# Later sums for two weights, and earlier copies out of one bank, in a hybrid attention and convolution layer

## The chip, the cores and the metric

The kernel runs on one core of a Trainium2 chip. Its engines are TensorE (PE, with PEld its weight loads), VectorE (DVE), ScalarE (ACT), GpSimd (POOL) and SyncE (SP); each runs its own instructions in a fixed order and waits on semaphores for the others. 16 DMA engines move data for all queues. The metric is the time of one execution in microseconds (us), the median of several runs.

## The reference

One layer on x of 512 tokens by 2048 channels, float32, cut to what matters:

```python
h = rmsnorm(x, g_pre)
q, k, v, z_att, u, g_glu, z_conv = split(h @ w_in)   # each 512 x 1024
# 8 heads x 128: stick-breaking attention, strictly causal
z = q k^T / sqrt(128)
a = exp(log_sigmoid(z) + sum over s<j<t of -softplus(z))
y_att = (a @ v) * silu(z_att)
# convolution module, 1024 channels
c = causal_depthwise_conv31(u * sigmoid(g_glu)) + conv_b
y_conv = (silu(layernorm(c)) @ w_pw2 + b_pw2) * silu(z_conv)
y = concat(y_att, y_conv) @ w_out                    # 2048 x 2048
out = x + rmsnorm(y, g_post)
```

## The kernel before

**Products.** Each float32 operand is split into an upper and a lower part (`split`, lines 101 to 111): ScalarE rounds a tile to its upper part (line 104), DVE subtracts (line 105). A product is three matmuls: upper by upper, upper by lower, lower by upper. Weights come in tiles of 1 MB: `r_` is the raw tile loaded by SyncE, `h_` its upper and `l_` its lower part, two buffers of each. A raw buffer is free for the load after next when DVE has made `l_`.

**Steps.** The work behind the start is a list of 96 steps, numbered from 0. A step has one weight tile and two units of matmuls; while a step runs, the next one's load and split are put into the program ahead of it. Steps 0 to 9 are u, q, k, g and u; 10 to 23 are v (12 matmuls in a unit); 24 to 49 are the rest of q, k, u, g and the gates za (24 matmuls in a unit), with the 8 heads of attention between their units; 50 to 63 are zc; 64 to 67 the pointwise product; 68 to 95 the output product. TensorE's order is written out by hand. The order on the other engines comes from a scheduler that places each instruction by its priority and by when it expects its inputs.

**Seven products for eight.** v, zc and the output product are cut in 2 x 2 blocks and done in 7 products in place of 8. Four of the seven need sums of weight blocks. GpSimd has them made in DRAM by DMA alone (`plan_sums`, lines 514 to 534): a transfer that copies one block (line 528) and one that accumulates another onto it (line 524). They are 1 MB each: 16 for v (`vs`), 16 for zc (`zs`) and 32 for w_out (`ws`). The last two lists are taken in turn from one queue, `sumq`.

**When a sum goes.** `sum_next` (line 536) issues the next transfer of a list and makes it wait for the latest matmul so far. For zc and w_out the constants of line 50 and these lines say how many are issued, at most one behind each unit:

```python
        if SUMS_FROM <= n < n_zc - 1 or n >= n_in:
            due += SUMS_A_STEP
```

Here n is the step, n_zc is 50 and n_in is 64. The queue of GpSimd is in order, so an instruction behind such a transfer waits until TensorE has come that far. Besides sums GpSimd runs the selects of attention (line 698, two groups of four for each head, `t1` and `t3`) that TensorE's transposes `aT` (line 742) need, additions of convolution channels (`ln_sum`, line 426) and small memsets.

**The end of v.** Steps 18 to 23 are the products 3, 7 and 4, in that order, two steps each; r_v30, r_v31, r_v70, r_v71, r_v40 and r_v41 are their weights. Products 7 and 4 use the same two PSUM banks, `va0` and `va1`. So when product 7 is done, `v_done` (line 608) has ScalarE copy each bank to SBUF (`v_a0`, `v_a1`, line 621), and TensorE may not begin product 4 in a bank before its copy is done. Step 24 is the first of q, with `r_q10`; step 25 has `r_q11`.

Of the kernel before, what the change touches and what calls it, by code (L numbers as in the profile page):

```python
# [46 lines left out]
    ("hl", 1), ("hl", 2), ("hl", 3),  # L47
]

SUMS_FROM, SUMS_A_STEP = 20, 1.5  # L50


@with_exitstack
def hybrid_layer(
# [15 lines left out]
    nc = tc.nc  # L70
# [18 lines left out]
    def t2(name, dt=F32):  # L89
        return t2p.tile([P, S], dt, tag="t2", name=name)  # L90
# [413 lines left out]
    def v_keep(chunk, m, src):  # L504
        a, b = t2(f"v_hi{chunk}_{m}", F32R), t2(f"v_lo{chunk}_{m}", F32R)
        v_hi[chunk, m], v_lo[chunk, m] = a, b
        split(a, b, src)
# [53 lines left out]
    v_form, v_ps, v_part = {}, {}, {}  # L561
# [46 lines left out]
    def v_done(q, i):  # L608
        ps = v_ps[q, i]
        tt = nc.vector.tensor_tensor  # L610
        if q in (1, 5, 6):
            v_part[q, i] = t2(f"v_part{q}_{i}")
            nc.scalar.copy(v_part[q, i], ps)
            return
        if q == 4:
            v_keep(0, 2 + i, ps)
            return
        c = v_part[{2: 1, 3: 6, 7: 5}[q], i]
        if q == 7:
            ps = t2(f"v_a{i}")  # L620
            nc.scalar.copy(ps, v_ps[q, i])
        if q == 2:
            tt(out=c, in0=ps, in1=c, op=ALU.add)
        elif q == 3:
            tt(out=c, in0=ps, in1=c, op=ALU.subtract)
        else:
            tt(out=c, in0=c, in1=ps, op=ALU.subtract)
        v_keep(0 if q == 2 else 1, i if q in (2, 3) else 2 + i, c)
# [18 lines left out]
    def v_unit(q, kg, i):  # L647
        def go(w):
            hi, lo = w
            if q == 2 and kg == 0:  # L650
                v_ps[q, i] = trp.tile([P, S], F32, tag="tr", name=f"vc{i}")
            elif kg == 0:
                v_ps[q, i] = {
                    1: lambda: mm(f"va{i}"), 5: lambda: mm(f"vb{i}"), 6: lambda: v_ps[1, i],
                    3: lambda: v_ps[5, i], 7: lambda: v_ps[1, i], 4: lambda: v_ps[1, i],
                }[q]()
            ps = v_ps[q, i]
            for k in range(4):
                ah, al = v_stationary(q, kg * 4 + k, i)
                st, en = q in (1, 2, 5) and kg + k == 0, kg == 1 and k == 3  # L660
                nc.tensor.matmul(ps, ah, hi[:, k, :], start=st, stop=False, skip_group_check=True)
                nc.tensor.matmul(ps, ah, lo[:, k, :], start=False, stop=False, skip_group_check=True)
                latest[0] = nc.tensor.matmul(
                    ps, al, hi[:, k, :], start=False, stop=en, skip_group_check=True
                ).ins
            if kg == 1:
                with tc.high_priority(offset=LATER):
                    v_done(q, i)
        return go
# [811 lines left out]
```

## Time and profile before

| | |
|---|---|
| median of 3 runs | 865.88 us (864.94 to 866.87) |
| the profiled execution | 864.89 us, of which its span is 863.2 |
| TensorE busy | 849.9 us (98%) |
| DVE, ScalarE, GpSimd busy | 658.0, 417.1, 142.8 us |
| mean granted TensorE clock | 0.996 |
| DMA queue of SyncE (q1) | 120.74 MB, 40.1% of 16 engines' span |
| DMA queue of GpSimd, the sums (q0) | 69.21 MB, 33.5% |

In a row of the order of time stand the start and the duration in us, engine, line, operation, output <- inputs, how many were merged, and in brackets how long the engine sat idle before it and what released it. Buffer numbers are left out of names there: `h_v` is any upper part of v's weights. A waits row reads: engine, tile and line that waited, what for, us in total, times, longest.

### The profile page before, as it was taken

What the parts mean: (1) busy time and instruction counts of PE and PEld (TensorE: products, weight loads), DVE (VectorE), ACT (ScalarE), POOL (GpSimd) and SP (SyncE); (2) the same over time, 40 slices, a digit from 0 to 9 for tenths busy, and PEclk for the clock granted to TensorE, in tenths of its full rate; (3) what the DMA queues carried; (4) which work ended last, traced back from release to release, by engine and by line L of the source; (5) the groups of instructions that cost most, each with busy time, mean ns of one, the idle gap of its engine ahead of it and who ended that gap; (6) DMA issues with size and microseconds to landing.
All of it is one profiled execution on the core that took longest, in us unless ns stands there. A gap on an engine that the chain in (4) does not pass through costs nothing.

```text
span 863.2 us, 9933 instructions
## 1 busy us (share of the span) xinstructions
PE 849.9 (98%) x3872; PEld 703.4 (81%) x3872; DVE 658.0 (76%) x791; ACT 417.1 (48%) x475; POOL 142.8 (17%) x170
## 2 busy tenths in 40 slices
PE   9999999999989999999999999999999999999996
PEld 6888888888868888888888888888888888888885
DVE  5799989689969669779898974368974776458774
ACT  5784222146444344333533545459853356455543
POOL 0111010200013131322313154230000100000031
PEclk9999999999999999999999999999999999999999
DMA  8798985856797889757698868937755995556783
GB/s 322 236 289 218 306 185 204 194 187 219 259 340 227 243 189 201 245 150 240 190 221 152 267 204 173 278 125 288 282 204 201 208 257 217 196 196 251 286 287 101
DMA packets 92278, 195.04 MB, mean 226 GB/s; under 512 B 3702, under 2 KB 46210, under 8 KB 86856
## 3 DMA queue, kind: packets, MB, share of 16 engines
q1 hardware_dynamic: 66688, 120.74, 40.1%
q0 software_dynamic: 22304, 69.21, 33.5%
q10 hardware_dynamic: 3240, 4.46, 1.6%
q8 instruction: 30, 0.49, 0.2%
q14 instruction: 16, 0.13, 0.0%
HBM read 186.01 MB, written 75.50 MB: 303 GB/s over the span
## 4 chain that ended last, share of the span: by engine, by line
PE 85%; DVE 8%; ACT 3%; DMA 2%; issue 1%; POOL 0%; DVEq 0%; ACTq 0%; POOLq 0%
PE q L353 3%; PE q L351 3%; PE q L352 3%; PE a L1091 3%; PE a L1092 3%; PE a L1090 3%; PE za L351 3%; PE za L353 3%; PE za L352 3%; PE u L351 3%; PE k L351 3%; PE k L353 3%; PE u L352 3%; PE k L352 3%; PE u L353 3%; DVE acc L410 2%
## 5 line engine op out<-in xcount | busy, mean ns | idle before, releaser
L410 DVE SCALAR_TENSOR_TENSOR acc<-hg,vec,acc 128x512 f32<-128x512 f32 x240 | 180.1, 750 | 6.6
L105 DVE TENSOR_TENSOR l_w<-r_w,h_w 128x2048 fp32r<-128x2048 f32 x28 | 64.2, 2292 | 42.2 <-ACT h_w L104 42.2
L104 ACT ACTIVATE h_w<-r_w 128x2048 fp32r<-128x2048 f32 x28 | 53.6, 1915 | 42.5 <-DMA r_w<-ws 12.7
L353 PE MATMUL q<-h_hi,l_q 128*128 128x512 f32 x128 | 50.8, 396 | 1.6 <-DVE l_q L105 1.6
L351 PE MATMUL q<-h_hi,h_q 128*128 128x512 f32 x128 | 50.6, 396 | 1.0 <-ACT h_q L104 1.0
L351 PE MATMUL u<-h_hi,h_u 128*128 128x512 f32 x128 | 50.3, 393 | 0.5 <-DVE k_lo L105 0.5
L352 PE MATMUL q<-h_lo,h_q 128*128 128x512 f32 x128 | 50.3, 393 | 0.0
L351 PE MATMUL k<-h_hi,h_k 128*128 128x512 f32 x128 | 50.1, 392 | 0.0
L351 PE MATMUL za<-h_hi,h_za 128*128 128x512 f32 x128 | 50.1, 391 | 0.0
L353 PE MATMUL k<-h_hi,l_k 128*128 128x512 f32 x128 | 49.9, 390 | 0.0
L353 PE MATMUL za<-h_hi,l_za 128*128 128x512 f32 x128 | 49.9, 390 | 0.0
L353 PE MATMUL u<-h_hi,l_u 128*128 128x512 f32 x128 | 49.9, 390 | 0.0
L352 PE MATMUL za<-h_lo,h_za 128*128 128x512 f32 x128 | 49.8, 389 | 0.0
L352 PE MATMUL k<-h_lo,h_k 128*128 128x512 f32 x128 | 49.8, 389 | 0.0
L352 PE MATMUL u<-h_lo,h_u 128*128 128x512 f32 x128 | 49.8, 389 | 0.0
L1092 PE MATMUL a<-h_w,f_lo 128*128 128x512 f32 x128 | 49.8, 389 | 0.0
L1091 PE MATMUL a<-l_w,f_hi 128*128 128x512 f32 x128 | 49.8, 389 | 0.0
L1090 PE MATMUL a<-h_w,f_hi 128*128 128x512 f32 x128 | 49.8, 389 | 0.0
L698 POOL TENSOR_SCALAR_AFFINE_SELECT t<-t 128x128 f32<-128x128 f32 x64 | 36.0, 596 | 74.2 <-DVE t L721 46.0
L105 DVE TENSOR_TENSOR l_z<-r_z,h_z 128x2048 fp32r<-128x2048 f32 x14 | 32.1, 2292 | 17.0 <-ACT h_z L104 16.9
L104 ACT ACTIVATE h_v<-r_v 128x2048 fp32r<-128x2048 f32 x14 | 26.8, 1915 | 37.2 <-PE u L352 17.5
L105 DVE TENSOR_TENSOR l_v<-r_v,h_v 128x2048 fp32r<-128x2048 f32 x14 | 33.0, 2361 | 13.0 <-ACT h_v L104 13.0
(381 smaller groups left out, 2246.5 us busy)
## 6 DMA issues: line engine op xcount, KB each, us to landing
ws<-in_w_out_dram POOLq DMA_DIRECT2D x24, 1024.0 KB, 9.6
r_w<-ws SPq DMA_DIRECT2D x16, 1024.0 KB
vs<-in_w_in_dram POOLq DMA_DIRECT2D x12, 1024.0 KB, 10.4
zs<-in_w_in_dram POOLq DMA_DIRECT2D x12, 1024.0 KB, 10.2
r_w<-in_w_out_dram SPq DMA_DIRECT2D x12, 1024.0 KB
r_u<-in_w_in_dram SPq DMA_DIRECT2D x8, 1024.0 KB
r_q<-in_w_in_dram SPq DMA_DIRECT2D x8, 1024.0 KB
r_k<-in_w_in_dram SPq DMA_DIRECT2D x8, 1024.0 KB
```

Source lines behind the costliest of these rows:

```text
L104: nc.scalar.activation(hi, src, AF.Copy)
L105: made = nc.vector.tensor_tensor(out=lo, in0=src, in1=f32(hi), op=ALU.subtract)
L351: nc.tensor.matmul(ps, wh, ah, start=first, stop=False)
L352: nc.tensor.matmul(ps, wh, al, start=False, stop=False)
L353: latest[0] = nc.tensor.matmul(ps, wl, ah, start=False, stop=last).ins
L410: bgq.append(lambda j=j: nc.vector.scalar_tensor_tensor(out=acc, in0=hg[:, j : j + S], scalar=vec[:, ct, j : j + 1], in1=acc, op0=ALU.mult ...
L698: nc.gpsimd.affine_select(out=blk, in_=blk, compare_op=ALU.is_gt, fill=0.0, base=0, pattern=[[-1, P]], channel_multiplier=1,)
L1090: nc.tensor.matmul(ps, fh[:, kk, ts], hi[:, k, :], start=st, stop=False, skip_group_check=True)
L1091: nc.tensor.matmul(ps, fh[:, kk, ts], lo[:, k, :], start=False, stop=False, skip_group_check=True)
L1092: nc.tensor.matmul(ps, fl[:, kk, ts], hi[:, k, :], start=False, stop=en, skip_group_check=True)
```

## The change

Two constants: the sums of zc and w_out begin with step 22 in place of 20, and 1.625 are due in a step in place of 1.5, which is 13 in 8 steps in place of 12. And the two copies v_a are given a high priority.

```diff
-SUMS_FROM, SUMS_A_STEP = 20, 1.5
+SUMS_FROM, SUMS_A_STEP = 22, 1.625
...
         if q == 7:
             ps = t2(f"v_a{i}")
-            nc.scalar.copy(ps, v_ps[q, i])
+
+            with tc.high_priority(offset=3000):
+                nc.scalar.copy(ps, v_ps[q, i])
```

The sums issued in a step, from line 1429 and at most one behind each unit:

| step | 20 | 21 | 22 | 23 | 24 | 25 | 26 | 27 | 28 | 29 | 30 | 31 |
|---|---|---|---|---|---|---|---|---|---|---|---|---|
| before | 1 | 2 | 1 | 2 | 1 | 2 | 1 | 2 | 1 | 2 | 1 | 2 |
| now | 0 | 0 | 1 | 2 | 1 | 2 | 2 | 1 | 2 | 2 | 1 | 2 |

By the end of step 48 both have issued 43; the last 5 follow from step 64 on.

GpSimd from the end of v's sums to the second head. `zs500` is the sum for product 5 of zc, first half of columns, first tile; `ws510` that of w_out, second half. Before:

```order
L524 DMA vs401_1274<-in_w_in_dram 512x1x512
L528 DMA zs500_1919<-in_w_in_dram 512x1x512
L528 DMA ws500_1960<-in_w_out_dram 512x1x512
L528 DMA zs501_1982<-in_w_in_dram 512x1x512
L528 DMA ws501_2003<-in_w_out_dram 512x1x512
L426 TENSOR_TENSOR ln_sum_1374<-ln_sum_1374,acc2_1433 128x512
L401 MEMSET hg4_2531 128x30
L524 DMA zs500_1919<-in_w_in_dram 512x1x512
L528 DMA ws510_2059<-in_w_out_dram 512x1x512
L524 DMA zs501_1982<-in_w_in_dram 512x1x512
L698 AFFINE_SELECT t1_0_2118<-t1_0_2118 128x128 x4
L528 DMA ws511_2206<-in_w_out_dram 512x1x512
```

Now, in the same place:

```order
L524 DMA vs401_1274<-in_w_in_dram 512x1x512
L426 TENSOR_TENSOR ln_sum_1374<-ln_sum_1374,acc2_1433 128x512
L401 MEMSET hg4_2529 128x30
L528 DMA zs500_1997<-in_w_in_dram 512x1x512
L528 DMA ws500_2035<-in_w_out_dram 512x1x512
L528 DMA zs501_2054<-in_w_in_dram 512x1x512
L528 DMA ws501_2099<-in_w_out_dram 512x1x512
L700 AFFINE_SELECT t1_0_2114<-t1_0_2114 128x128 x4
L524 DMA zs500_1997<-in_w_in_dram 512x1x512
L700 AFFINE_SELECT t3_0_2115<-t3_0_2115 128x128 x4
L528 DMA ws510_2235<-in_w_out_dram 512x1x512
```

The addition and the memset have moved ahead of the first sum, and three sums that stood ahead of head 0's first selects now stand behind them.

ScalarE at the end of v, from the first copy out of product 7's banks to the splits of q's first two weights. Before:

```order
L621 COPY v_a0_1953<-va0_1477 128x512
L104 ACTIVATE v_hi1_2_1956<-v_part5_0_1693 128x512
L104 ACTIVATE h_v41_1986<-r_v41_1985 128x2048
L621 COPY v_a1_1975<-va1_1491 128x512
L104 ACTIVATE v_hi1_3_1978<-v_part5_1_1708 128x512
L104 ACTIVATE h_q10_2020<-r_q10_2019 128x2048
L104 ACTIVATE v_hi0_2_2037<-va0_1477 128x512
L104 ACTIVATE h_q11_2074<-r_q11_2073 128x2048
```

Now:

```order
L623 COPY v_a0_1951<-va0_1477 128x512
L104 ACTIVATE v_hi1_2_1954<-v_part5_0_1693 128x512
L104 ACTIVATE h_v41_1980<-r_v41_1979 128x2048
L623 COPY v_a1_1971<-va1_1491 128x512
L104 ACTIVATE v_hi1_3_1974<-v_part5_1_1708 128x512
L104 ACTIVATE h_q10_2014<-r_q10_2013 128x2048
L104 ACTIVATE v_hi0_2_2031<-va0_1477 128x512
L104 ACTIVATE h_q11_2069<-r_q11_2068 128x2048
```

Nothing moved here: only line and buffer numbers differ. TensorE's and SyncE's rows are the same throughout as well. On DVE the lower part of a weight trades places with the scans of a head (line 729, now 731) in heads 1, 4 and 5, and in 4 and 5 one small operation goes ahead of the head's subtraction (line 733, now 735).

## The prediction

> **What bounds the kernel now.** I read the page first, then the list of waits for TensorE, then the stretch of the program where most of that waiting lies: TensorE, ScalarE, GpSimd and the SyncE queue in order of time, and last the traffic of the DMA queues microsecond by microsecond.
>
> ```profile
> span 863.2 us, 9933 instructions
> PE 849.9 (98%) x3872; PEld 703.4 (81%) x3872; DVE 658.0 (76%) x791; ACT 417.1 (48%) x475; POOL 142.8 (17%) x170
> PE idle L1284 <- POOL mean_w L140: 1.8, 1, 1.8
> PE va L661 <- ACT v_a L621: 1.7, 1, 1.7
> PE q L353 <- DVE l_q L105: 1.6, 1, 1.6
> PE last L1160 <- ACT diag L1159: 1.5, 1, 1.5
> PE q L351 <- ACT h_q L104: 1.0, 1, 1.0
> PE u L351 <- DVE k_lo L105: 0.5, 1, 0.5
> ```
>
> TensorE is busy for 98% of the span, so only its own waits can shorten the kernel, and there are six. The first and the fourth are the program's start and its last block. Three of the other four (v_a, h_q, l_q) lie within 12 us of each other, where the last two steps of v pass into the first step of q:
>
> ```profile
> 236.34 0.39 PE L661 MATMUL va<-h_v,h_hi 128*128 128x512 f32 x1
> 238.83 0.39 PE L663 MATMUL va<-h_v,h_lo 128*128 128x512 f32 x1
> 240.88 0.50 PE L661 MATMUL va<-h_v,h_hi 128*128 128x512 f32 x1 [1.66 <-ACT v_a L621]
> 250.36 0.50 PE L351 MATMUL q<-h_hi,h_q 128*128 128x512 f32 x1 [1.03 <-ACT h_q L104]
> 252.69 0.79 PE L353 MATMUL q<-h_hi,l_q 128*128 128x512 f32 x1 [1.59 <-DVE l_q L105]
> 253.28 0.63 PE L351 MATMUL q<-h_hi,h_q 128*128 128x512 f32 x1
> 253.71 0.63 PE L352 MATMUL q<-h_lo,h_q 128*128 128x512 f32 x1
> 256.40 0.39 PE L353 MATMUL q<-h_hi,l_q 128*128 128x512 f32 x1
> ```
>
> From start to start a product takes (238.83 - 236.34) / 11 = 0.226 us here. Between 238.83 and 256.40 stand 48 products (three units of v of 12, and 12 of q), which is 10.87 us at that pace and took 17.57. So this place loses **6.7 us**: 240.88 - 238.83 - 0.23 = 1.8 us at v_a, and 4.9 us at h_q, l_q and in the products behind them, which come 0.43 us apart (253.28 to 253.71) before the pace returns. Why were they late?
>
> ```profile
> 230.28 0.32 SPq L639 DMA_DIRECT2D r_v<-vs  x1
> 235.42 0.38 SPq L336 DMA_DIRECT2D r_q<-in_w_in_dram  x1
> 236.03 0.63 ACT L104 ACTIVATE v_hi<-v_part 128x512 fp32r<-128x512 f32 x1 [1.62 <-DVE v_part L627]
> 238.44 1.91 ACT L104 ACTIVATE h_v<-r_v 128x2048 fp32r<-128x2048 f32 x1 [1.78 <-DMA r_v<-vs]
> 240.26 0.57 ACT L621 COPY v_a<-va 128x512 f32<-128x512 f32 x1
> 248.40 1.91 ACT L104 ACTIVATE h_q<-r_q 128x2048 fp32r<-128x2048 f32 x1 [3.45 <-DMA r_q<-in_w_in_dram]
> ```
>
> Both roots are loads. The last weights of v were issued at 230.28 and split from 238.44 on; the copy v_a that TensorE needs stood behind that split on ScalarE. The first weights of q were issued at 235.42 and split from 248.40, 13 us later. What lay between are the sums that GpSimd issues:
>
> ```profile
> 228.65 0.76 POOL L528 DMA_DIRECT2D zs<-in_w_in_dram  x1 [61.38 <-PE va L663]
> 234.09 0.73 POOL L528 DMA_DIRECT2D ws<-in_w_out_dram  x1 [4.68 <-PE va L663]
> 236.80 0.70 POOL L528 DMA_DIRECT2D zs<-in_w_in_dram  x1 [1.98 <-PE va L663]
> 239.52 0.70 POOL L528 DMA_DIRECT2D ws<-in_w_out_dram  x1 [2.02 <-PE va L663]
> 240.15 1.37 POOL L426 TENSOR_TENSOR ln_sum<-ln_sum,acc 128x512 f32<-128x512 f32 x1
> ```
>
> The DMA view of single microseconds shows who moved data (packets, MB, share of the 16 engines). The rows are those of the microsecond from 231 (one), 234 (one), 237 (two), 240 (its larger one), 243 (two); q0 carries the sums, q1 SyncE's loads.
>
> ```profile
> q0 software_dynamic: 94, 0.39, 95.3%
> ...
> q1 hardware_dynamic: 47, 0.39, 104.0%
> ...
> q0 software_dynamic: 96, 0.39, 97.4%
> q1 hardware_dynamic: 5, 0.02, 5.9%
> ...
> q1 hardware_dynamic: 357, 0.37, 102.6%
> ...
> q0 software_dynamic: 97, 0.38, 92.6%
> q1 hardware_dynamic: 42, 0.04, 10.7%
> ```
>
> They take turns, nearly whole: the load of v issued at 230.28 gets nothing in 231, all of 234, and its last packets wait in 237 behind the second sum; the load of q gets 240 and then a tenth of 243. A load alone is 1.05 MB / 0.37 to 0.39 MB per us = 2.7 to 2.8 us.
>
> **The change, part by part.** *Copies.* The two v_a copies are to be moved ahead on ScalarE. ScalarE's rows at this place are the same in both programs: the second copy still stands behind the split of the last weights of v. This part adds, removes and moves nothing; cost and gain 0. If the wait at v_a goes, it goes because the load is early.
>
> *Sums, start.* By the two constants, steps 20 to 23 issued 1, 2, 1 and 2 sums and now issue 0, 0, 1 and 2. A unit of v is 2.7 us, so the first sum moves from 228.65 to the end of the first unit of step 22, 239.06, the second to about 244.5, the third to 247.2, the fourth into the first step of q. The 228.65, 234.09 and 236.80 transfers are then gone from the time in which both late loads run.
>
> - Load of v, issued 230.28 as before (its buffer comes free by DVE, which is untouched): alone it lands near 234 to 235. Its split may then start when ScalarE is done with v_hi, at 236.03 + 0.63 = 236.66, not 238.44. Everything behind shifts by 1.78 us: TensorE resumes at 240.88 - 1.78 = 239.10, where its own pace asks for 239.06. Bounds: 0 to 1.8 us remain; I take 0.05, since no sum stands in front of the load any more.
> - Load of q, issued 235.42: alone about 3 us and a start of one or two, so 239 to 241; at worst 248.4 as before. The nearest row is that of 240, the load alone, since the first sum is now issued after it. ScalarE reaches h_q at about 242.1 (it must first split a part of v that waits for DVE), then 1.9 and 2.3 us for h_q and l_q: 246.4. TensorE comes to q at 239.06 + 3 x 2.72 = 247.2 and needs l_q 0.45 us later. Covered by 1 us; if the load landed later than 243 that cover is gone.
> - The products at 0.43 us come only behind the waits, so they go with them. The Trainium skill, "TensorE: Matmul & The Clock Gate" (What's actually happening), says that the array halves its clock after an idle window of about 3.4 us and regains it after as long a busy one. The 0.43 us rows agree, and so does the single wait at 240.88 without them; by that rule a remaining wait of 1 or 2 us would cost itself and no slow stretch.
>
> *Sums, rate.* 13 in 8 steps for 12: by step 48 both programs have issued 43. In between each comes up to two and a half steps later, and nobody reads one before the steps of zc. A copy moves 0.39 MB in a microsecond, 2.7 us; an accumulation half of that:
>
> ```profile
> q0 software_dynamic: 96, 0.20, 109.2%
> 252.66 6.19 SPq L336 DMA_DIRECT2D r_k<-in_w_in_dram  x2
> 266.71 1.92 ACT L104 ACTIVATE h_k<-r_k 128x2048 fp32r<-128x2048 f32 x1 [1.38 <-PE q L352]
> ```
>
> (the row is of the microsecond from 252, an accumulation: 5.2 us for a sum). Per step of about 12 us that is 2.8 us of load and 1.5 sums of 2.7 to 5.2 us, now 1.6: under 11.3 us. The load of k issued at 252.66 was wanted at 266.71, when TensorE freed the buffer, 14 us later, and had landed by then although the four sums shown above were issued in the 24 us ahead of it. Loads in these steps have twice the room of v's. Cost 0, hidden by that room.
>
> *GpSimd's queue.* The addition ln_sum moves from behind the fourth sum to ahead of the first, so from 240.15 to about 237, when DVE has finished its input. There it no longer runs beside l_v, which took 3.29 us; beside the small v_lo it meets nothing that TensorE waits for. The selects of each head now stand behind other sums. A sum holds the queue until TensorE has passed its unit, so I compared that unit with the time each select is ready: for all 16 groups the unit ends first, by under 1 us at the closest. Head 0's second group, the first to get an accumulation ahead of it, is ready near 270.4, and that sum is let go near 265.6.
>
> ```profile
> 277.02 3.18 POOL L698 TENSOR_SCALAR_AFFINE_SELECT t<-t 128x128 f32<-128x128 f32 x4 [3.37 <-ACT t L734]
> 283.06 1.14 PE L742 MATMUL aT<-ident,t 128*128 128x128 f32 x9
> 240.39 3.29 DVE L105 TENSOR_TENSOR l_v<-r_v,h_v 128x2048 fp32r<-128x2048 f32 x1 [2.99 <-ACT h_v L104]
> ```
>
> *DVE.* In heads 1, 4 and 5 a weight's lower part changes places with scans. That costs a head at most the rest of a split and one operation of 512 columns, an estimate of 1.5 us from the 1.91 and 0.63 of such on ScalarE. Head 0 had 283.06 - 280.20 = 2.9 us to spare ahead of its transposes, and I take the others to be like it. In head 0 TensorE no longer waits while DVE catches up, so DVE is there about 1 us later relative to TensorE (two l of 2.3 us and 13 taps have to follow each other); that still fits. What is late next is k_lo (0.5 us), which stays.
>
> **Sum.** 6.7 - 0.05 - 0.05 for rounding = 6.6 us. The profiled execution took 864.89 us, its span 863.2 and 1.7 around it; 864.9 - 6.6 = 858.3. It lay 1.0 us under the median of the three runs, 865.88, so the median should be **859.3 us**, 0.76% faster. A measurement of this kernel can tell about 0.2%, 1.7 us.
>
> **Rivals.**
> 1. *v_a still waits.* The copy has not moved, so any lateness of v's last load or its split keeps the 1.8 us: 859.3 + 1.8 = 861.1. For it: the 1.78 us is TensorE's to lose at the least delay. Against it: the rows of 231 and 237, where the sums alone hold the load up. The Trainium skill, "DMA: Bandwidth & Descriptors" (Queues, rings and completion order), says that each engine goes round-robin between its queues packet by packet. By an even share the load of v would have landed near 237 beside the sums, in time for ScalarE, the 1.8 us would have another cause, and the sum would be 861.1; the rows of 231 and 234 speak against an even share.
> 2. *DVE is the next bound.* TensorE arrives 6.6 us earlier, DVE only in part: if head 0's chain slips by 5 us instead of 1, its transposes wait 2 us: 861.3. Against it: DVE waited 2.99 us at 240.39, idleness that it gets back.
> 3. *The wait moves to q.* If the first sum at 239.06 still cuts off the tail of q's load, 4.9 us stay and only 1.8 go: 864.1, at the edge of no change; with 1 us more elsewhere, none. Against it: 3.6 us between the two issues, where the load needs 2.8.
> 4. *Slower.* The denser accumulations (five in steps 28 to 31) make loads late within attention. A late load there costs what q's did, 4.9 us; two make 859.3 + 9.8 = 869.1. It decides when a load lands some 20 us after its issue (14 us to the split, 6 more to its use), so three accumulations of 5.2 us and its own 2.8 in a row do not reach it; their units lie 5.4 us or more apart.
>
> **Chances.** Forecast 0.63; rival 1 0.12; rival 2 0.10; rival 3 0.09; rival 4 0.06. Faster by over 0.2%: the forecast, rivals 1 and 2 and a third of rival 3, 0.88. Same: the rest of rival 3, 0.06. Slower 0.06. The range goes from 857.9 (k_lo's 0.5 also gone, and a low run) to 862.5, past rivals 1 and 2 and short of 3 and 4.
>
> **What would show it.** In the changed kernel's waits v_a, h_q and l_q are gone or under 0.3 us each; q0 is silent until about 240; v's last split starts near 236.7, and q's first near 242; no products 0.43 us apart; ScalarE's order as before. The step most likely to be wrong is q's load landing by 243, or a transpose of a head that now waits for a select on GpSimd: either would stand as a new row among TensorE's waits.

## The result, and the profile after

The changed kernel takes **857.71 us** (median of 4 runs, 857.53 to 858.60), the kernel before in the same series 866.18 us (4 runs, 864.94 to 866.87). The ratio is **0.9906**, with a 95% interval of 0.9889 to 0.9923: 8.5 us faster (6.7 to 9.6), where 6.6 were forecast. The time lies 1.6 us under the 859.3 us that were forecast, and 0.2 us under the lower end of the forecast's range, 857.9. (The kernel before came out at 866.18 us here, 0.3 us above the 865.88 from which the forecast started.) The profiled execution of the changed kernel took 858.60 us.

First the head of the page, then TensorE's waits:

```profile
span 856.9 us, 9933 instructions
PE 847.4 (99%) x3872; PEld 702.0 (82%) x3872; DVE 654.3 (76%) x791; ACT 416.8 (49%) x475; POOL 146.4 (17%) x170
PE idle L1286 <- POOL mean_w L140: 1.8, 1, 1.8
PE last L1162 <- ACT diag L1161: 1.5, 1, 1.5
PE gn L493 <- ACT h_hi L252: 0.7, 1, 0.7
PE u L351 <- DVE k_lo L105: 0.5, 1, 0.5
```

The rows of v_a, h_q and l_q are gone. The row of gn is new; it lies in the program's start, 21 us in (e1 below has 0.4 us there, the others none), and it shifts everything in this execution by some 0.7 us. So the rows that follow stand about 0.75 us later than rows of before would. In order of time, SyncE's queue, ScalarE and GpSimd at the end of v and the start of q:

```profile
231.03 0.32 SPq L641 DMA_DIRECT2D r_v<-vs  x1
236.16 5.83 SPq L336 DMA_DIRECT2D r_q<-in_w_in_dram  x2
236.77 0.63 ACT L104 ACTIVATE v_hi<-v_part 128x512 fp32r<-128x512 f32 x1 [1.62 <-DVE v_part L629]
237.33 1.92 ACT L104 ACTIVATE h_v<-r_v 128x2048 fp32r<-128x2048 f32 x1
239.16 0.56 ACT L623 COPY v_a<-va 128x512 f32<-128x512 f32 x1
242.87 1.92 ACT L104 ACTIVATE h_q<-r_q 128x2048 fp32r<-128x2048 f32 x1
249.79 1.92 ACT L104 ACTIVATE h_q<-r_q 128x2048 fp32r<-128x2048 f32 x1 [3.60 <-DMA r_q<-in_w_in_dram]
237.54 1.74 POOL L426 TENSOR_TENSOR ln_sum<-ln_sum,acc 128x512 f32<-128x512 f32 x1 [69.51 <-DVE acc L410]
240.27 0.76 POOL L528 DMA_DIRECT2D zs<-in_w_in_dram  x1 [0.93 <-PE va L665]
```

The split of v's last weights follows v_hi at once, and the first split of q's weights has no brackets: neither waits for its load now. The copy v_a still stands behind the split, as before, and is early enough. The queues, in the microseconds from 234, 239, 240, 241 and 243:

```profile
q1 hardware_dynamic: 53, 0.42, 98.6%
...
q1 hardware_dynamic: 369, 0.38, 107.6%
...
q1 hardware_dynamic: 194, 0.18, 52.1%
...
q0 software_dynamic: 13, 0.05, 46.4%
...
q0 software_dynamic: 100, 0.41, 102.4%
```

Both loads have the engines to themselves, and the first packets of a sum come in 241, when q's load is through. TensorE passes the place at its pace of 0.23 us, without the products 0.43 us apart:

```profile
247.83 0.39 PE L665 MATMUL va<-h_v,h_lo 128*128 128x512 f32 x1
248.06 0.39 PE L351 MATMUL q<-h_hi,h_q 128*128 128x512 f32 x1
248.51 0.39 PE L353 MATMUL q<-h_hi,l_q 128*128 128x512 f32 x1
```

### The profile page after: what moved, and what is told of

It is laid out like the page before. It is cut to its first block, busy times and chain, and to the rows that moved or that the text cites. A ratio compares the mean times of both kernels' runs of the same rounds, so it can differ in the third digit from the quotient of the medians.

```text
span 856.9 us, 9933 instructions
## 1 busy us (share of the span) xinstructions
PE 847.4 (99%) x3872; PEld 702.0 (82%) x3872; DVE 654.3 (76%) x791; ACT 416.8 (49%) x475; POOL 146.4 (17%) x170
## 4 chain that ended last, share of the span: by engine, by line
PE 90%; DVE 5%; ACT 2%; DMA 2%; issue 1%; SPq 0%; DVEq 0%; ACTq 0%
PE za L351 3%; PE za L353 3%; PE za L352 3%; PE q L352 3%; PE a L1094 3%; PE a L1093 3%; PE q L351 3%; PE q L353 3%; PE a L1092 3%; PE u L351 3%; PE k L351 3%; PE k L353 3%; PE u L353 3%; PE u L352 3%; PE k L352 3%; DMA r_gn<-in_w_in_dram 2%
```

## The experiments

The theory: the sums' traffic makes two loads late, and the start at step 22 takes it out of their way. Its rivals: the copies did it; GpSimd's queue did it (the addition ln_sum now stands ahead of the sums); the wait at v_a was a loss of its own, set by ScalarE's order. The first four ran on one chip (before: 865.12 us, 863.21 to 867.41, 23 runs), the others on a second (before: 864.62 us, 861.42 to 867.99, 23 runs).

**e1, the copies alone.**

```diff
-SUMS_FROM, SUMS_A_STEP = 22, 1.625
+SUMS_FROM, SUMS_A_STEP = 20, 1.5      # the changed kernel, with the constants of before
```

> Only the priority of the two v_a copies is changed; the sums begin with step 20 at 1.5 a step. Theory (the sums' start is the whole gain, the copies' part moves no instruction): the time of the kernel before, 866 us within 0.2%, with the three waits at v_a, h_q and l_q of its profile, 6 to 9 us with the slow products. Rival (the copies bring the v_a part): 864.3 us or less and no wait at v_a. Second use: the changed kernel gained 8.5 us between the medians, where the forecast's sum from one execution said 6.6; if the place loses more here than the 6.7 us of that execution, its size varies from run to run and the execution read was a mild one.

Measured: 864.55 us (861.73 to 866.43, 12 runs), ratio 0.999 (0.9976 to 1.0003). TensorE's waits in it:

```profile
PE q L353 <- DVE l_q L105: 1.6, 1, 1.6
...
PE va L663 <- ACT v_a L623: 0.9, 1, 0.9
PE q L351 <- ACT h_q L104: 0.6, 1, 0.6
...
PE va L664 <- DVE l_v L105: 0.4, 1, 0.4
```

All three waits are there, those of v_a and h_q smaller in this execution. The place loses 4.6 us here, less than the 6 to 9 that were expected, because the products behind the waits are not slow this time (the last section says why). The priority given to the copies brings nothing by itself.

**e2, the later start alone.**

```diff
-SUMS_FROM, SUMS_A_STEP = 22, 1.625
+SUMS_FROM, SUMS_A_STEP = 22, 1.5      # the changed kernel, with the rate of before
```

> Start with step 22, rate left at 1.5 a step, so 40 sums by step 48 in place of 43 and 8 behind step 64. Theory (the start is the gain, the rate only makes up for it): 857.7 us within 0.2%, no wait at v_a, h_q or l_q. Rival (the closer sums matter, by loads that are late in the steps of attention or, the other way, by late sums): away from the changed kernel by over 1.7 us; if the three sums pushed behind step 64 collide with the output weights, slower by one late load, some 5 us.

Measured: 870.30 us (868.81 to 870.91, 6 runs), ratio 1.0049 (1.0033 to 1.0065): slower than before by 5 us, and than the changed kernel by 12.6. The waits at v and q are gone; two larger ones stand in the output product:

```profile
PE a L1092 <- ACT h_w L104: 8.3, 1, 8.3
...
PE a L1093 <- DVE l_w L105: 1.5, 1, 1.5
```

Without the higher rate three more sums are left for the time behind step 64. Of its last four accumulations the first and the last two, the load of output weights issued behind them, and that load's split:

```profile
685.36 1.21 POOL L524 DMA_DIRECT2D ws<-in_w_out_dram  x1 [5.22 <-PE pw L353]
...
695.98 2.31 POOL L524 DMA_DIRECT2D ws<-in_w_out_dram  x2 [4.27 <-PE pw L353]
699.81 0.38 SPq L1014 DMA_DIRECT2D r_w<-in_w_out_dram  x1
718.38 1.91 ACT L104 ACTIVATE h_w<-r_w 128x2048 fp32r<-128x2048 f32 x1 [9.71 <-DMA r_w<-in_w_out_dram]
```

The load takes 18.6 us to its split. In the changed kernel the last sum is issued at 680.07, and the same load, issued at 700.22, is split here:

```profile
680.07 1.16 POOL L524 DMA_DIRECT2D ws<-in_w_out_dram  x1 [4.30 <-PE pw L353]
705.20 1.92 ACT L104 ACTIVATE h_w<-r_w 128x2048 fp32r<-128x2048 f32 x1 [0.27 <-DMA r_w<-in_w_out_dram]
```

From TensorE's last product ahead of the first wait, at 711.62, to 726.98, where the pace is back, stand 12 products. At their pace these are 2.7 us, and they took 15.4: 12.6 us are lost, all that e2 takes more than the changed kernel. The rival that the expectation named came: the three sums collide with the output weights.

So the later start is what takes the three waits away, and the rate is what keeps it from costing more than that, some 450 us later.

**e4, the three early issues put back, small.** In the changed kernel GpSimd issues three transfers of 8 KB, to a place that nobody reads, behind the units where the sums of steps 20 and 21 stood before.

```diff
+            if (n, units_done % 2) in ((20, 1), (21, 1), (21, 0)):
+                spare = dram.tile([P, 4, S], F32, name=f"spare{units_done}")
+                tc.add_manual_dep(
+                    nc.gpsimd.dma_start(spare[:16, 0, :128], w_block(0, 0, 0, 0)[:16, 0, :128]).ins, latest[0].name,
...
```

> The changed kernel with three more transfers of 8 KB issued by GpSimd at the gates of the old first three sums (steps 20, 21, 21) into a scratch tensor. GpSimd's queue is held there as before the change, and ln_sum stands behind them. Theory (the traffic of the sums delays the loads): 857.7 us within 0.2%, none of the three waits. Rival (what counts is GpSimd's queue: the issue itself, or ln_sum beside DVE's l_v): a good part of the 8.5 us comes back, 861 to 866.

Measured: 857.80 us (857.69 to 857.93, 5 runs), ratio 0.9909 (0.9895 to 0.9924), the time of the changed kernel. All its TensorE waits:

```profile
PE idle L1286 <- POOL mean_w L140: 1.8, 1, 1.8
PE last L1162 <- ACT diag L1161: 1.5, 1, 1.5
PE u L351 <- DVE k_lo L105: 0.5, 1, 0.5
```

GpSimd waits at the same gates again (it issues at 228.59, 234.03 and 236.75, before at 228.65, 234.09 and 236.80), ln_sum stands behind them, and nothing is lost: holding GpSimd's queue costs nothing by itself.

**e5, the three early issues put back, whole.** As e4, with 1 MB each.

```diff
-                    nc.gpsimd.dma_start(spare[:16, 0, :128], w_block(0, 0, 0, 0)[:16, 0, :128]).ins, latest[0].name,
+                    nc.gpsimd.dma_start(spare, w_block(0, 0, 0, 0)).ins, latest[0].name,
```

> The same with three whole copies of 1 MB from w_out into scratch at those gates, so 3 MB more traffic than any other kernel here. Theory: the three waits are back, since the last load of v and the first of q again run beside three copies: v_a 1.5 to 2 us, h_q and l_q 3 to 7 us with the slow products, 863 to 867 us. Rival (GpSimd's queue and not the traffic): the same time as with the small ones.

Measured: 865.87 us (863.25 to 867.30, 12 runs), ratio 1.0002 (0.9991 to 1.0013). The waits are back:

```profile
PE q L353 <- DVE l_q L105: 1.6, 1, 1.6
PE q L351 <- ACT h_q L104: 1.6, 1, 1.6
...
PE va L663 <- ACT v_a L623: 1.1, 1, 1.1
```

The edits of e4 and e5 differ only in the bytes, 3 x 8 KB and 3 x 1 MB, and the times by 8.1 us. The traffic is the cause.

One thing came back with the traffic. In e4 ln_sum runs at 237.25 and is over when DVE makes l_v; in e5 it runs at 240.55, beside l_v, which takes longer there (e4 first, then e5):

```profile
238.49 2.29 DVE L105 TENSOR_TENSOR l_v<-r_v,h_v 128x2048 fp32r<-128x2048 f32 x1 [1.16 <-ACT h_v L104]
240.26 3.82 DVE L105 TENSOR_TENSOR l_v<-r_v,h_v 128x2048 fp32r<-128x2048 f32 x1 [2.47 <-ACT h_v L104]
```

This is too little to be a rival for the 8 us. In the kernel before, where l_v takes 3.29 us, no product comes late for it; in e5 one comes 0.3 us late, in e1 0.5.

**e6, before with the copy ahead on ScalarE.** Does the wait at v_a go if the copy stands ahead of the split of v's last weights, which the priority in the change did not bring about?

```diff
-            nc.scalar.copy(ps, v_ps[q, i])
+            bank_free[i] = nc.scalar.copy(ps, v_ps[q, i]).ins
...
+            if (q, kg) == (4, 1):     # the split of r_v41, written out, its upper part after the copy of bank 1
+                upper = nc.scalar.activation(hi, raw, AF.Copy)
+                tc.add_manual_dep(upper.ins, bank_free[1].name, ...)
```

> The kernel before, sums from step 20 at 1.5, with the second v_a copy really ahead of the split of v's last weights on ScalarE (a dependency added, so the order does move). Theory (the loads set the end of this place): the wait at v_a goes, but q's first load lands no earlier, so TensorE waits the 1 to 2 us longer at h_q and l_q: the time of the kernel before within 0.2%. Rival (the v_a wait is a loss of its own, as the forecast's rival 1 priced it): 1 to 1.9 us faster, about 863.5.

Measured: 864.53 us (862.14 to 866.75, 12 runs), ratio 1.0 (0.9985 to 1.0015). The copy now runs at 236.65 and the split at 238.17, and TensorE waits elsewhere:

```profile
236.65 0.57 ACT L621 COPY v_a<-va 128x512 f32<-128x512 f32 x1
238.17 1.92 ACT L642 ACTIVATE h_v<-r_v 128x2048 fp32r<-128x2048 f32 x1 [0.95 <-DMA r_v<-vs]
...
PE va L674 <- DVE l_v L648: 1.6, 1, 1.6
```

The waits at l_q (1.6 us) and h_q (1.0 us) are as in before. The 1.7 us of v_a have become 1.6 us of l_v, where the expectation had them at h_q and l_q. Most of these 1.6 us are not the load's: l_v takes 3.66 us in e6, beside ln_sum at 240.25, and 2.29 in e4, so 1.4 us of the wait go with GpSimd's work beside it.

The time stays all the same, and the row that says why is q's first split. It waits for its load until 248.37, as in before (248.40):

```profile
248.37 1.91 ACT L104 ACTIVATE h_q<-r_q 128x2048 fp32r<-128x2048 f32 x1 [7.76 <-DMA r_q<-in_w_in_dram]
```

By these rows, what TensorE saved ahead of that split it would wait for behind it. So the wait at v_a is no loss of its own: the late load of q ends this place, whatever ScalarE's order.

**e7, a start at step 21, and e8, a start at step 24.** How much of the delay is needed, and does more bring more? The rates are set so that as many sums are issued by step 48.

```diff
-SUMS_FROM, SUMS_A_STEP = 22, 1.625
+SUMS_FROM, SUMS_A_STEP = 21, 1.5625   # e7
+SUMS_FROM, SUMS_A_STEP = 24, 1.75     # e8
```

> Sums from step 21 at 1.5625 (43 by step 48). The first sum goes at about 234, so v's last load (issued 230) is free of sums and q's first (issued 235.4) has one copy of 2.7 us ahead of it and the next one at 239 to share with. Theory: no wait at v_a; q's load lands 3 to 6 us later than in the changed kernel, at 243 to 246, where the cover was to end at 243: 857.7 to 862 us. Rival (a threshold of the whole place, or other causes): as before, 865, or all gained, 857.7.

Measured: 858.72 us (858.10 to 860.28, 4 runs), ratio 0.9938 (0.9916 to 0.9959). Its first sum is issued at 234.08. The load of v still comes in time. That of q's first weights, which the expectation had 3 to 6 us late, delays its split by 0.6 us, and TensorE does not wait for it. It is q's second load that is late, as the second split shows, and behind it the transposes of head 0 wait for GpSimd's selects:

```profile
242.70 1.92 ACT L104 ACTIVATE h_q<-r_q 128x2048 fp32r<-128x2048 f32 x1 [0.61 <-DMA r_q<-in_w_in_dram]
253.35 1.92 ACT L104 ACTIVATE h_q<-r_q 128x2048 fp32r<-128x2048 f32 x1 [7.91 <-DMA r_q<-in_w_in_dram]
...
PE aT L744 <- POOL t L700: 1.6, 3, 1.0
```

> Sums from step 24 at 1.75 a step (43 by step 48). Theory: with step 22 nothing was left to win at this place, and the denser sums still leave the loads of attention their room: 857.7 us within 0.2%. Rival (denser sums make loads late, the forecast's rival 4): a new wait on a weight's split in steps 28 to 48, 5 us or more each.

Measured: 857.88 us (857.59 to 859.84, 4 runs), ratio 0.9933 (0.9908 to 0.9957), and no TensorE wait but the three that e4 has. Its first sum comes at 253.02 and q's second split at 247.36, with no wait for its load; in e7 that split stands 6.0 us later. From step 22 on there is nothing left to win here.

**e3, the rate alone.**

```diff
-SUMS_FROM, SUMS_A_STEP = 22, 1.625
+SUMS_FROM, SUMS_A_STEP = 20, 1.625
```

> Start left at step 20, rate 1.625 (47 sums by step 48, so only one is left behind step 64). Theory: the waits at v_a, h_q and l_q stay, 863 to 867 us; the rate brings nothing by itself. Rival (the rate is part of the gain, since fewer accumulations meet the loads of w_out): 1 us or more faster than the kernel before without a change at v_a, h_q and l_q.

Measured: 865.13 us (863.08 to 867.35, 10 runs), ratio 1.0009 (0.9994 to 1.0024). The three waits stay (l_q 1.6, v_a 1.3, h_q 1.0 us). The rate alone neither gains nor costs.

No version beats the changed kernel by more than the runs scatter. TensorE's waits that are left, 1.8, 1.5 and 0.5 us, lie outside what these constants reach.

## Why the prediction was right, point by point

**The mechanism.** This is what was right; one term of the sum was mis-sized (below). Each of its marks came: the three waits gone, q0 silent until the microsecond from 241, the split of v's last weights at 237.33 - 0.75 = 236.6 (236.66 forecast), that of q at 242.87 - 0.75 = 242.1 (242.1 forecast), no products at 0.43 us, ScalarE's order unchanged. e4 and e5 show that the traffic, not the issues, was the cause. The forecast priced the wait at v_a, 1.8 us, as a loss beside those at q; by e6 it is none of its own, since the load of q ends the place. The 6.7 us are right all the same, because both loads became early together.

**The size.** For each profiled execution I added up how much later than 0.2267 us after the last one each product starts, from the last two steps of v through the first of q, and took it from the time:

| kernel | profiled execution, us | lost at this place | the rest |
|---|---|---|---|
| before | 864.89 | 6.7 | 858.2 |
| e1, copies alone | 862.84 | 4.6 | 858.3 |
| e3, rate alone | 864.09 | 6.4 | 857.7 |
| e5, 1 MB put back | 865.36 | 7.2 | 858.2 |
| e6, copy ahead | 864.60 | 6.6 | 858.0 |
| changed kernel | 858.60 | 0.1 | 858.5 |
| e4, 8 KB put back | 857.84 | 0.1 | 857.8 |
| e8, start at 24 | 857.59 | 0.1 | 857.5 |

The rest is the same within 1.0 us. The 6.7 us of the sum were right for the execution they were read from.

**What was mis-sized: the step from that execution to the median, +1.0 us.** The forecast took the profiled execution, 864.89, as 1.0 us lower than typical, and carried the 1.0 over to the changed kernel. Over 23 runs each, in two other series, the median of before is 865.12 and 864.62, so the execution was typical and the three runs shown were high. And what differs between the executions of the table, one of each kernel, is mostly the loss itself, 4.6 to 7.2 us, so an offset of before had no place in a kernel without that loss. (Only profiled executions have a trace; the other runs' losses were not seen.) Without that step the forecast is 858.3 and its range 856.9 to 861.5, and 857.71 was measured. The last 0.6 has one shown part: before lost 0.4 us in zc in that execution, at a place which no row of the waits names, and the changed kernel does not:

```profile
616.65 0.39 PE L887 MATMUL zb<-h_z,zf_hi 128*128 128x512 f32 x1
617.16 0.50 PE L888 MATMUL zb<-l_z,zf_hi 128*128 128x512 f32 x1
617.50 0.39 PE L889 MATMUL zb<-h_z,zf_lo 128*128 128x512 f32 x1
```

(0.51 and 0.34 us from start to start, in place of 0.23 each). e1, e3 and e6, which make their sums from step 20 as before does, do not show it either (e2, whose sums come last, has 0.3 us there), so I count it as this execution's and not as the change's. The other 0.2 us is within the scatter. Of the 8.5 us between the two medians shown, then, some 7 seem to be the change, and the rest the few runs of before: e4, which has the time of the changed kernel, against the 23 runs beside it gives 865.12 - 857.80 = 7.3.

**The clock.** The forecast held that a wait of 1 or 2 us that remains would cost itself and bring no slow stretch. Its own rows say otherwise: ahead of the products 0.43 us apart stand waits of 1.03 and 1.59 us, 2.6 us together, while 1.66 us alone brought none. This did not reach the sum, because the waits went. The last section works out what counts.

**The copies, cost and gain 0:** right, by e1.

**The rate, cost 0:** right as a difference to before (e3), but this treated the rate as an extra that must not hurt. e2 shows what it is for: without it the three deferred sums end in front of the output weights. The forecast noted that both programs have issued 43 sums by step 48; it did not ask what the place behind step 64 could bear.

**Rival 1** (v_a waits by itself) falls: the copy stands where it stood in the changed kernel, and the wait is gone; and by e6 the time is not the wait's to give. **Rival 2** (head 0's transposes) did not come at step 22, but e7 has its wait one step earlier, 1.6 us when q's second split stands 6.0 us later than in e8. That DVE's chain carries the one to the other is argued, not shown. The changed kernel has part of that lateness too (ScalarE sits idle for 3.60 us until this load, at 249.79; in e4 the same split comes at 248.87, 1.5 us later than in e8), and it stays covered. **Rival 3** did not come: the first sum's packets begin after q's load. **Rival 4** (accumulations in a row make a load late) did not come in attention, and is what e2 does in the output product; "a load lands some 20 us after its issue" was its condition, and there its split came 18.6 us after the issue.

## What to carry to other kernels

When a wait names an engine, look one step back for a load, and ask what else was on the DMA queues between its issue and its landing: transfers that nobody needs for a long time cost TensorE several microseconds here, because they were issued beside one that was needed in 10 us. A wait that you see is not yet a gain: ask what would end the place if it went. Deferred transfers have to be made up before the next tight place, so start and rate are one choice. And a difference between the profiled execution and the median is not an offset to carry over, before one knows whether the place that the change removes is what varies.

## What the runs showed of the hardware

**What a load gets beside a sum differed from place to place.** Beside a copy from DRAM to DRAM, the load of q got 0.04 MB in the microsecond from 243 of the kernel before, and the copy 0.38. Beside an accumulation, in the microsecond from 714 of e2:

```profile
q0 software_dynamic: 64, 0.13, 70.4%
q1 hardware_dynamic: 64, 0.13, 39.2%
```

Here they take turns one for one, and both are slow: the load has 0.13 MB in a microsecond where a load alone has 0.37 to 0.42, so 1.05 MB takes 8 us. The Trainium skill, "DMA: Bandwidth & Descriptors" (Queues, rings and completion order), says that an engine goes round-robin between its queues, a packet at a time. The 64 and 64 of e2 agree with an even share; the 97 and 42 beside a copy, with 0.38 and 0.04 MB, do not.

It is not simply copy against accumulation. In the microsecond from 254 of before an accumulation runs, the load of k had been issued at 252.66, and the view's list of queues has one row:

```profile
q0 software_dynamic: 105, 0.22, 112.7%
```

The load got nothing, though in the changed kernel the load of q, issued at 236.16, had moved 110 packets by 238. The loads differ too: a packet of q's is 1 KB (0.04 MB in 42), of e2's 2 KB (0.13 MB in 64). No run here separates these, and what sets the share stays open.

**DVE and GpSimd side by side.** The lower part of a tile of v's weights took DVE 2.29 us in the five traces where ln_sum was over by then (the changed kernel, e2, e4, e7, e8), and 3.29 to 4.05 us in the five where GpSimd ran ln_sum beside it (before, e1, e3, e5, e6).

**The runs of some kernels scatter more than those of others.** The kernels whose early sums meet the two loads spread over 4.1 to 6.6 us (before 4.2 in 23 runs and 6.6 in 23, e1 4.7, e3 4.3, e5 4.1, e6 4.6); those without spread over 0.2 to 2.3 us (e4 0.2, the changed kernel 1.1, e8 2.3), in fewer runs. Part of it goes with the clock. Of the 23 runs of before on the second chip, the five with a mean granted clock of 0.998 or 0.999 took 861.42 to 862.82 us, and the 13 with 0.997 took 862.44 to 866.09, 864.8 in the mean. One slow stretch, 3.4 us at half clock in 863, is 0.002 of the mean clock.

**TensorE's slow stretch goes by windows of 3.41 us.** In e1 the waits of 0.61 us at h_q and 1.59 us at l_q, 2.3 us apart, left the products behind them at 0.23 us. In e3 the waits were 1.01 and 1.59, and:

```profile
250.10 0.50 PE L351 MATMUL q<-h_hi,h_q 128*128 128x512 f32 x1 [1.01 <-ACT h_q L104]
...
252.43 0.80 PE L353 MATMUL q<-h_hi,l_q 128*128 128x512 f32 x1 [1.59 <-DVE l_q L105]
...
255.84 0.40 PE L352 MATMUL q<-h_lo,h_q 128*128 128x512 f32 x1
```

From 252.43 to 255.84 stand 8 products in 3.4 us, 0.43 us each, and 1.6 us were lost on top of the waits. The Trainium skill, "TensorE: Matmul & The Clock Gate" (What's actually happening), puts the throttle down to an idle window of about 3.4 us and its release to as long a busy one. The length of the stretch agrees; the idleness ahead of it, 2.6 us in two pieces with two products between them, is less than that window.

The traces' records of the granted clock show what counts. After its first rise the clock changes only at whole multiples of 3.413 us: in before it rises at 6.88, falls to half at 252.64, which is 72 of these windows later, and rises at 256.05, one window on. In the ten traces, the clock was at half behind every window in which TensorE's records leave 1.84 us or more idle (19 windows), and behind none with 1.66 us or less; no window lies between. Half a window is 1.71 us. In e3 both waits fall into one window, with 2.36 us idle. In e1 a window ends at 251.95, in the middle of the second wait, and it has 1.50 us. By these figures it is the place of the windows that decides whether two such waits bring a slow stretch; no run here moves the windows alone.
